# The delta rule's gate taken into the scan, and the scan's norm folded into its transposition

## The chip, the cores and the metric

The kernel runs on one core of a Trainium2 chip. The time is the device time of one launch in microseconds, the median over runs. The core has five engines with queues of their own, each worked through strictly in order: PE (TensorE: matmuls and transpositions), DVE (VectorE), ACT (ScalarE), POOL (GpSimd) and SP, which here only issues DMAs (ACT issues some as well). Engines wait for each other through semaphores. Matmul results land in PSUM, eight banks of 128x512 fp32; everything else lives in SBUF or, where it is parked, in DRAM.

## The reference, cut to what matters

One layer of a generator over 256 latent and 256 context tokens of width 1024: a SwiGLU half step, a mixer, a second half step, a last norm. The change is in the mixer, which runs a gated delta rule (8 heads of 128, both directions) and a Mamba-2 state-space scan (SSD, 32 heads of 64 in two groups) on one input projection, and merges them:

```python
def mixer_out(f, o, y, ...):
    ya = rmsnorm(o, gdn_norm_g) * silu(za)                  # delta rule: norm and gate
    yb = (y + mb_d * xs) * silu(zB)                         # SSD: skip and gate
    yb = rmsnorm(yb, mb_norm_g)                             # per group of 1024 channels
    merged = sigmoid(ga) * (ya @ w_branch_gdn) + sigmoid(gb) * (yb @ w_branch_mb)
    return merged @ w_out
```

## The kernel before

The program is written as a list of steps (`PLAN`), each with a priority; a scheduler at build time puts the instructions of each engine into one fixed order by priority, by readiness in its own timing model and by free buffers. What stands on a queue stays in that order on the chip. A step that comes earlier in `PLAN` is also served first when buffers of a pool are handed out; a lower number ahead of a step is more urgent.

Weight products are done as three fp32r matmuls of split operands: `unit` loads 512 KB of weights into one of four `raw` buffers (SP), casts the high part `whi` (ACT, L197) and subtracts for the low part `wlo` (DVE, L201); `mm3` (L212 to L214) multiplies. Projections whose input is `hF` run as plain fp32 matmuls (L648, L1165) straight from `raw`.

The steps that matter, in the order of `PLAN`:

- `zB1`, `zA9`, `zB4`: gate projections as plain fp32 matmuls. `zA_gen` makes eight tiles `zth` (L648 on PE, L1178 on ACT, L1179 on DVE) and parks each in DRAM as `zAsc`. `zB_gen` makes four blocks `zbt` (L1165, L1168, L1169), parked as `zsc`.
- `h40` is `ssd_all`, the scan, four quarters (two groups, two halves). Per quarter `ssd_off` loads `xlat`, starts `y` as skip term (L1455) and adds four products `pyo` through `yo` (L1466 to L1472); `ssd_diag`, twice, builds an 8x128 decay matrix in `Es` (POOL L1501, DVE L1503, ACT L1505), a second one B (L1509 on ACT or L1511 on DVE, by `DGB`, then L1514), multiplies both (L1516) and sends them through PE as `pyd` (L1519, added in L1520); `ssd_gate` loads the parked `zt`, multiplies (L1528) and squares on ACT with a row sum (L1529). After each second quarter `ssd_norm` makes the factor `yr` and scales `y` in four passes (L1540).
- `y0`, `y1` are `ssd_out`: `y` is transposed on PE into `pyb` (L1574, one PSUM bank), the norm's gain applied and the result split into `ybH` (ACT, L1578) and `ybL` (DVE, L1579).
- `gdn_out`: the normed delta-rule output `o` is transposed (`pya`, L1400), multiplied with the loaded `zA` (L1405), split into `yaH` (ACT) and `yaL` (POOL, L1407), and goes through eight projections with `wbg`, 24 matmuls each.
- `mb_out`: eight projections of both `yb` groups with `wbm`, then `w_out`.

Of the kernel before, what the change touches and what calls it, by code (L numbers as in the profile page):

```python
# [8 lines left out]
AF = mybir.ActivationFunctionType  # L9
ALU = mybir.AluOpType  # L10
# [4 lines left out]
P = 128  # L15
D = 1024
KD = 8
NL = 256
# [10 lines left out]
T4 = 2  # L29
NCV = 2  # L30
PLAN = """10/k3 block_decay k6 18/v3 13/dts 18/g2 20/v2 g3 row_scale 5/elim 20/g10 v4 21/gdn_rows dts_rows 13/m0 14/m1 13/chain_start s0 s1 m2 m3 22/q9
    B_part 27/x17 25/lat_h 22/C_part 30/g17 chain_out 13/s2 s3 14/gdn_norm 15/ssd_pre 30/zB1 zA9 zB4 15/h40 51/y0 gdn_out y1 70/mb_out"""
NG = 5
GQ = 0
EST = ("t4", "tt")
# [4 lines left out]
F2T, W2L, HUT = ["mm", "mm", "mg", "mg", "tr", "ch"], "dve", "tZ"  # L40
CBT = "n8"
WAT = [("tt", "tt"), ("tt", "tt"), ("c4", "c4"), ("ring", "ring"), ("s4", "s4"), ("s4", "s4"), ("tt", "tt"), ("c4", "c4")]
DGA, DGB, DGM = "g", "av", "v"
PYD = ("sd", "tr")
XDT = "c4"
YOT = 'tA'
# [90 lines left out]
class Kernel:  # L137
# [1249 lines left out]
        for t in range(2):  # L1387
            V.tensor_tensor(o[t], o[t], bc(rs[:, t], 8, P), op=ALU.mult)

    def gdn_out(self):  # L1390

        nc, V = self.nc, self.nc.vector
        o, bc = self.o, self.bc
        yH = Ks(self, 8, NL, "yaH")
        yL = Ks(self, 8, NL, "yaL")
        for h2 in range(4):
            pv = self.smp([P, 2, NL], "pya", "ch")
            for j in range(2):
                for t in range(2):
                    nc.tensor.transpose(pv[:, j, t * P:t * P + P], o[t][:, 2 * h2 + j], self.ident)  # L1400
            ya = self.t2([P, 2, NL], "ya")
            j, hs = h2 // 2, slice(2 * (h2 % 2), 2 * (h2 % 2) + 2)
            zA = self.t2([P, 2, NL], "zA", tag="tL")
            nc.sync.dma_start(zA, self.zAsc[2 * h2:2 * h2 + 2].rearrange("m p n -> p m n"))
            V.scalar_tensor_tensor(out=ya, in0=pv, scalar=self.gng, in1=zA, op0=ALU.mult, op1=ALU.mult)  # L1405
            nc.scalar.copy(yH.t[j][:, hs], ya)
            (V if YAL[h2] == "v" else nc.gpsimd).tensor_tensor(yL.t[j][:, hs], ya, yH.t[j].bitcast(F32)[:, hs], op=ALU.subtract)  # L1407
        mg = self.mg = Ks(self, 8, NL, "mg", F32)
        for m in range(8):
            acc = self.proj("wbg", m, yH, yL, NL)  # L1410
            ga = self.t2([P, NL], "ga", tag="tL")
            nc.sync.dma_start(ga, self.gsc[m])
            V.scalar_tensor_tensor(out=mg[m], in0=ga, scalar=1.0, in1=acc, op0=ALU.add, op1=ALU.mult)
# [117 lines left out]
    def ssd_norm(self, gi):  # L1531
        V = self.nc.vector
        r = self.const([P, 2], f"yr{gi}")
        V.tensor_tensor(r, self.rsum[:, :, gi, 0], self.rsum[:, :, gi, 1], op=ALU.add)

        self.rsqrt(r, r, 1.0 / 1024, 4 * EPS)
        for hf in range(2):
            y = self.yx[gi, hf][0]
            for t in range(2):
                V.tensor_scalar(out=y[:, t], in0=y[:, t], scalar1=r[:, t:t + 1], scalar2=None, op0=ALU.mult)  # L1540

    def ssd_all(self):

        self.yx = {}
        self.v3 = lambda ap: ap.rearrange("p (h c) -> p h c", c=64)
        self.b64 = lambda ap: ap.rearrange("p (h o) -> p h o", o=1).to_broadcast([P, ap.shape[1], 64])
        qs = [(gi, hf) for gi in range(2) for hf in range(2)]
        self.ssd_off(*qs[0])
        yield
        for n, q in enumerate(qs):  # L1550
            for i in range(2):
                self.ssd_diag(*q, i)
                yield
                yield
                if i == OFA and n < 3:
                    self.ssd_off(*qs[n + 1])
                    yield
            self.ssd_gate(*q)
            if q[1]:
                self.ssd_norm(q[0])  # L1560
            yield

    def ssd_out(self, gi):

        nc, V = self.nc, self.nc.vector
        y = [self.yx[gi, hf][0] for hf in range(2)]
        yH = Ks(self, 8, NL, f"ybH{gi}")
        yL = Ks(self, 8, NL, f"ybL{gi}")
        for c2 in range(4):
            pv = self.smp([P, 2, NL], "pyb", "tr")  # L1570
            for j in range(2):
                c = 2 * c2 + j
                for t in range(2):
                    nc.tensor.transpose(pv[:, j, t * P:t * P + P], y[c // 4][:, t, (c % 4) * P:(c % 4) * P + P], self.ident)  # L1574
            for j in range(2):
                c = 2 * c2 + j
                g = self.mbg[:, 8 * gi + c:8 * gi + c + 1]
                nc.scalar.activation(yH[c], pv[:, j], AF.Identity, scale=g)  # L1578
                V.scalar_tensor_tensor(out=yL[c], in0=pv[:, j], scalar=g, in1=yH[c].bitcast(F32), op0=ALU.mult, op1=ALU.subtract)  # L1579
        self.yb.append((yH, yL))  # L1580
# [124 lines left out]
```

## Time and profile before

| | us |
|---|---|
| median of 3 runs | 1290.8 (1288.43 to 1293.3) |
| the profiled execution, its own time | 1292.01 |
| its span in the trace | 1290.3 |
| PE busy | 1247.7 (97%) |
| DVE busy | 954.3 (74%) |
| ACT busy | 481.3 (37%) |
| POOL busy | 98.8 (8%) |
| mean granted TensorE clock | 0.981 |

The times of the profile are microseconds from the span's start. Busy is the union of an engine's instructions; a matmul's end is modelled, so that neighbours overlap a little. The stretch of the change lies between 865 us, where the first `zA` projections run, and 1016 us, where `mb_out` starts. Plain fp32 matmuls are recorded in two passes, so that one of them counts as two in the trace; transpositions and fp32r matmuls count once.

### The profile page before, as it was taken

The numbers are of one execution on the slowest core, as the hardware profiler recorded it, in microseconds if no ns is written. First come the engines' busy times: TensorE is split into PE (matmuls) and PEld (weight loads), VectorE is DVE, ScalarE is ACT, GpSimd is POOL, SyncE is SP. The second block draws the span as 40 slices with busy tenths as digits, with TensorE's granted clock in tenths as the row PEclk, the third lists the DMA queues.
The fourth block names the chain that finished last, engine by engine and source line by source line (L and its number), as shares of the span: only waits on it lengthen the run. The fifth ranks groups of instructions, "written<-read, shape, count | busy, mean of one in ns | idle before, by whom it ended". The sixth has DMA issues, their size and how long they took to land.

```text
span 1290.3 us, 21033 instructions
## 1 busy us (share of the span) xinstructions
PE 1247.7 (97%) x8042; PEld 1088.3 (84%) x8042; DVE 954.3 (74%) x1748; ACT 481.3 (37%) x919; POOL 98.8 (8%) x119
## 2 busy tenths in 40 slices
PE   9999999999999999998989999999996999999997
PEld 8888888888899888888978799867545999999997
DVE  5997586646667995888786798948896566866565
ACT  4321222212236663144323554422224445543443
POOL 1000000000010140100110211100111002000000
PEclk9999999999998999999999999999997999999998
DMA  9566367636632388885541456668655565555552
GB/s 366 181 221 212 115 222 240 206 129 219 214 104 106 107 202 201 263 249 163 158 121 50 143 176 192 198 201 291 221 178 168 188 224 180 196 193 180 181 183 78
DMA packets 138132, 239.41 MB, mean 186 GB/s; under 512 B 41072, under 2 KB 81456, under 8 KB 137904
## 3 DMA queue, kind: packets, MB, share of 16 engines
q1 hardware_dynamic: 98688, 214.32, 51.1%
q10 hardware_dynamic: 39344, 23.76, 6.2%
q8 instruction: 63, 1.03, 0.3%
q14 instruction: 37, 0.30, 0.1%
HBM read 211.72 MB, written 26.31 MB: 184 GB/s over the span
## 4 chain that ended last, share of the span: by engine, by line
PE 61%; issue 16%; DVE 12%; DMA 7%; ACT 2%; SPq 1%; POOL 0%; POOLq 0%; DVEq 0%; ACTq 0%
PE acc L213 16%; PE acc L212 16%; PE acc L214 16%; PE acc L648 3%; DVE wlo L201 1%; DVE cv L667 1%; DVE Es L1503 1%; PE acc L1165 1%; PE pada L318 1%; DVE Es L1514 1%; PE pn L1343 1%; DMA vsc<-vt 1%; DVE N L1056 1%; DVE etmp L1053 1%; DMA raw<-in_wgs 1%
## 5 line engine op out<-in xcount | busy, mean ns | idle before, releaser
L197 ACT CAST whi<-raw 128x1024 fp32r<-128x1024 f32 (+1 forms) x208 | 214.5, 1034 | 454.9 <-PE acc L213 374.8
L213 PE MATMUL acc<-hL,whi 128*128 128x512 f32 (+1 forms) x976 | 345.1, 354 | 0.5 <-DVE hL L468 0.5
L214 PE MATMUL acc<-hH,wlo 128*128 128x512 f32 (+1 forms) x976 | 344.5, 353 | 0.0
L212 PE MATMUL acc<-hH,whi 128*128 128x512 f32 (+1 forms) x976 | 339.9, 355 | 0.9 <-ACT cv L665 0.5
L201 DVE TENSOR_TENSOR wlo<-raw,whi 128x1024 fp32r<-128x1024 f32 (+1 forms) x208 | 250.7, 1207 | 73.8 <-ACT whi L197 72.2
L212 PEld LDWEIGHTS acc<-hH,whi 128*128 128x128 f32 x976 | 186.1, 191 | 24.7 <-ACT cv L665 1.1
L213 PEld LDWEIGHTS acc<-hL,whi 128*128 128x128 f32 x976 | 186.6, 191 | 23.9 <-DVE hL L468 0.9
L214 PEld LDWEIGHTS acc<-hH,wlo 128*128 128x128 f32 x976 | 186.5, 191 | 23.3
L290 DVE CUSTOM_DVE_ANT_0 junk<-wadat,cs 128x1024 f32<-128x1024 f32 x80 | 97.8, 1222 | 43.5 <-DMA wadat<-in_wadaT 42.6
L213 PE MATMUL acc<-aL,whi 128*128 128x256 f32 (+1 forms) x384 | 122.9, 323 | 0.0
L214 PE MATMUL acc<-aH,wlo 128*128 128x256 f32 (+1 forms) x384 | 122.3, 323 | 0.0
L212 PE MATMUL acc<-aH,whi 128*128 128x256 f32 (+1 forms) x384 | 122.2, 323 | 0.0
L667 DVE SCALAR_TENSOR_TENSOR cv<-cbuf,cc,cv 128x512 f32<-128x512 f32 (+1 forms) x144 | 97.9, 690 | 8.8 <-ACT cv L665 7.2
L648 PE MATMUL acc<-hF,raw 128*128 128x256 f32 x416 | 93.1, 380 | 1.9 <-DMA raw<-in_wg 1.7
L648 PEld LDWEIGHTS acc<-hF,raw 128*128 128x128 f32 x416 | 78.2, 190 | 14.9 <-issue 2.4
L213 PEld LDWEIGHTS acc<-aL,whi 128*128 128x128 f32 x384 | 73.0, 190 | 5.7
L212 PEld LDWEIGHTS acc<-aH,whi 128*128 128x128 f32 x384 | 72.6, 190 | 5.7
L214 PEld LDWEIGHTS acc<-aH,wlo 128*128 128x128 f32 x384 | 72.7, 190 | 5.5
L604 DVE SCALAR_TENSOR_TENSOR xl<-acc,hg,xl 128x256 f32<-128x256 f32 x64 | 30.3, 482 | 47.3 <-PE acc L214 46.8
L1165 PE MATMUL acc<-raw,hF 128*128 128x512 f32 x128 | 58.3, 607 | 0.0
L1165 PEld LDWEIGHTS acc<-raw,hF 128*128 128x128 f32 x128 | 24.7, 195 | 29.9 <-issue 29.6
L401 POOL TENSOR_TENSOR sqa<-sqa,sqb 128x256 f32<-128x256 f32 x12 | 11.3, 945 | 455.4 <-ACT sqb L399 452.6
(403 smaller groups left out, 1971.8 us busy)
## 6 DMA issues: line engine op xcount, KB each, us to landing
raw<-in_wgu SPq DMA_DIRECT2D x76, 512.0 KB, 4.0
wadat<-in_wadaT SPq DMA_DIRECT2D x56, 512.0 KB, 4.1
raw<-in_wdn SPq DMA_DIRECT2D x44, 512.0 KB, 3.4
wada<-in_wada SPq DMA_DIRECT2D x16, 512.0 KB, 9.6
raw<-in_wg SPq DMA_DIRECT2D x16, 512.0 KB, 4.6
Es<-asd SPq DMA_DIRECT2D x16, 512.0 KB, 4.4
raw<-in_wxs SPq DMA_DIRECT2D x16, 512.0 KB, 3.7
raw<-in_wzB SPq DMA_DIRECT2D x16, 512.0 KB, 3.9
```

What stands on the lines that cost most here:

```text
L197: nc.scalar.copy(hi, raw)
L201: engs[i % len(engs)].tensor_tensor(lo[:, c:c + w], raw[:, c:c + w], hi[:, c:c + w].bitcast(F32), op=ALU.subtract)
L212: mm(acc, wh, xh, start=start, stop=False)
L213: mm(acc, wh, xl, start=False, stop=False)
L214: mm(acc, wl, xh, start=False, stop=stop)
L290: self.nc.vector.tensor_tensor_reduce(out=self.junk, in0=w, in1=self.cs[s], scale=1.0, scalar=0.0, op0=ALU.mult, op1=ALU.add, accum_out=out)
L318: mm = lambda c, q: nc.tensor.matmul(pa[:, c], loads[k][c][:, q * P:q * P + P], self.cTs[:, q:q + 1].to_broadcast([P, P // 2, 2]), start=q ...
L604: nc.vector.scalar_tensor_tensor(out=xs, in0=acc[:, NL * s - g0:NL * s - g0 + NL], scalar=hg[s][:, m:m + 1], in1=xs, op0=ALU.mult, op1=ALU ...
L648: self.nc.tensor.matmul(acc, w[:, k * P:k * P + P], self.hF[:, k], start=k == 0, stop=k == KD - 1)
L667: nc.vector.scalar_tensor_tensor(out=u3, in0=buf[:, 0:R, j:j + 64], scalar=cw[:, j:j + 1], in1=u3, op0=ALU.mult, op1=ALU.add)
L1053: V.tensor_tensor(tmp, N[:, :, k + 1:32, k:k + 1].to_broadcast([P, 2, nr, k]), N[:, :, k:k + 1, 0:k].to_broadcast([P, 2, nr, k]), op=ALU.mult)
L1165: nc.tensor.matmul(accs[t], self.hF[:, k, sl], w[:, wsl], start=k == 0, stop=k == 7)
```

## The change

Four edits. `gdn_out` is cut in two: `gdn_pre` (transposition, gate and split of the delta rule's output) moves to a place between `zA9` and `zB4` in `PLAN`, ahead of the scan `h40`; the eight projections keep the name `gdn_out` and come after `y1`. The scan's norm no longer scales `y` on DVE: `ssd_norm` makes a diagonal matrix `ydg` of the factors on ACT, and `ssd_out` multiplies `y` with it instead of transposing against the identity, so that scaling and transposition are one plain fp32 matmul. `pyb` alternates between two PSUM banks. And all eight B matrices are started on ACT (`DGB` is "a" and not "av").

```diff
-    ... 30/zB1 zA9 zB4 15/h40 51/y0 gdn_out y1 70/mb_out"""
+    ... 30/zB1 zA9 29/gdn_pre 30/zB4 15/h40 51/y0 y1 60/gdn_out 70/mb_out"""
-DGA, DGB, DGM = "g", "av", "v"
+DGA, DGB, DGM = "g", "a", "v"
@@ def gdn_out(self), now gdn_pre up to the split of ya
-    def gdn_out(self):
+    def gdn_pre(self):
         yH = Ks(self, 8, NL, "yaH")
         yL = Ks(self, 8, NL, "yaL")
+        self.ya = yH, yL
...
+    def gdn_out(self):
         mg = self.mg = Ks(self, 8, NL, "mg", F32)
         for m in range(8):
-            acc = self.proj("wbg", m, yH, yL, NL)
+            acc = self.proj("wbg", m, *self.ya, NL)
@@ def ssd_norm(self, gi)
         self.rsqrt(r, r, 1.0 / 1024, 4 * EPS)
-        for hf in range(2):
-            y = self.yx[gi, hf][0]
-            for t in range(2):
-                V.tensor_scalar(out=y[:, t], in0=y[:, t], scalar1=r[:, t:t + 1], scalar2=None, op0=ALU.mult)
+        dg = self.t2([P, 2, P], "ydg", tag="tM")
+        for t in range(2):
+            self.nc.scalar.activation(dg[:, t], self.ident, AF.Copy, scale=r[:, t:t + 1])
+        self.ydg[gi] = dg
@@ def ssd_out(self, gi)
-            pv = self.smp([P, 2, NL], "pyb", "tr")
+            pv = self.smp([P, 2, NL], "pyb", ("tr", "sd")[c2 % 2])
...
-                    nc.tensor.transpose(pv[:, j, t * P:t * P + P], y[c // 4][:, t, (c % 4) * P:(c % 4) * P + P], self.ident)
+                    nc.tensor.matmul(pv[:, j, t * P:t * P + P], y[c // 4][:, t, (c % 4) * P:(c % 4) * P + P], self.ydg[gi][:, t],
+                                     start=True, stop=True)
```

The scheduler makes a new order of it. Three places of it follow; in the changed kernel line numbers past L1390 are some 5 to 7 higher.

DVE, where the scan starts, before: the start of `y` (L1455), the first `yo` and the first decay matrices stand between the gates `zth` of the `zA` projections.

```order
L1169 SCALAR_TENSOR_TENSOR zbt<-zbt,acc 128x512 x2
L1455 TENSOR_TENSOR yg<-xlat,mbD 128x512 x2
L1471 TENSOR_TENSOR yo<-pyo,cbm 128x512
L1132 TENSOR_TENSOR sst<-pSs,egm 128x256
L1472 TENSOR_TENSOR yg<-yg,yo 128x512
L1179 SCALAR_TENSOR_TENSOR zth<-zth,acc 128x256 x2
L1437 TENSOR_TENSOR cbm<-pcb,UT 128x2x128
L1511 TENSOR_TENSOR Es<-cbm,dt 128x1024
```

DVE at the same place now: the gate of the delta rule (`ya`, L1406) stands behind the `zth`, and all of `yo` and `yg` behind `ya`.

```order
L1179 SCALAR_TENSOR_TENSOR zth<-zth,acc 128x256 x2
L1406 SCALAR_TENSOR_TENSOR ya<-pya,cc,zA 128x512 x2
L1179 SCALAR_TENSOR_TENSOR zth<-zth,acc 128x256
L1406 SCALAR_TENSOR_TENSOR ya<-pya,cc,zA 128x512 x2
L1476 TENSOR_TENSOR yo<-pyo,cbm 128x512 x2
L1460 TENSOR_TENSOR yg<-xlat,mbD 128x512 x2
L1477 TENSOR_TENSOR yg<-yg,yo 128x512 x2
L1460 TENSOR_TENSOR yg<-xlat,mbD 128x512 x2
```

What moved: every `yo` and `yg` of the scan is now queued behind the last `ya`, which needs the last two of the eight `zA` tiles back from DRAM.

SP's DMA queue, before, around the first weights of `zA`: three of the four `xlat` loads stand ahead of the `zA` weights.

```order
L1453 DMA xlat<-xsc 128x2x512
L638 DMA raw<-in_wBC 128x1024
L1450 DMA Sm<-ssc 128x2x512
L638 DMA raw<-in_wg 128x1024
L1450 DMA S_7930<-ssc 128x2x512
L1488 DMA Es<-asd 128x1024
L638 DMA raw<-in_wzB 128x1024
L1453 DMA xlat<-xsc 128x2x512 x2
```

SP's queue now, behind the last weights of `zA`: the loads of `zA` back from DRAM and the `xlat` loads behind them.

```order
L638 DMA raw<-in_wzA 128x1024
L1493 DMA Es<-asd 128x1024
L638 DMA raw<-in_wzB 128x1024
L1405 DMA zA<-zAsc 128x2x256
L638 DMA raw<-in_wzB 128x1024 x2
L1405 DMA zA<-zAsc 128x2x256
L638 DMA raw<-in_wzB 128x1024
L1405 DMA zA<-zAsc 128x2x256
L1458 DMA xlat<-xsc 128x2x512
L1532 DMA zt<-zsc 128x512 x2
L1458 DMA xlat<-xsc 128x2x512 x2
```

What moved: all four `xlat` loads are issued behind the last load of `zA`, which waits for the store of the eighth tile.

PE at the scan's end, before: the last zB matmuls and the last scan products `pyd`, then the transpositions `pya` and `pyb`, then the first `wbg` matmuls.

```order
L1165 MATMUL acc<-raw,hF 128x512
L1519 MATMUL pyd<-xlat,Es 128x64 x16
L1165 MATMUL acc<-raw,hF 128x512 x23
L1519 MATMUL pyd<-xlat,Es 128x64 x16
L1400 MATMUL pya<-ident,o_7186 128x128
L1400 MATMUL pya<-ident,o_7187 128x128
L1400 MATMUL pya<-ident,o_7186 128x128
```

PE there now: 48 `wbg` matmuls, two of the eight projections, are threaded between the last scan products; behind the last `pyd` come all eight groups of `pyb` in one row, then the other six projections.

```order
L212 MATMUL acc<-yaH,whi 128x256
L213 MATMUL acc<-yaL,whi 128x256
L214 MATMUL acc<-yaH,wlo 128x256
L1524 MATMUL pyd<-xlat,Es 128x64 x16
L1580 MATMUL pyb<-ydg,yg 128x128 x32
L212 MATMUL acc<-yaH,whi 128x256
L213 MATMUL acc<-yaL,whi 128x256
L214 MATMUL acc<-yaH,wlo 128x256
```

What moved: before, the second group's `pyb` were spread between `wbg` and `wbm` matmuls that covered their splitting; now 144 `wbg` matmuls wait on PE's queue behind both groups' `pyb`.

More of the change, by code (lines that the diff above doesn't have):

```diff
@@ L31 @@
 PLAN = """10/k3 block_decay k6 18/v3 13/dts 18/g2 20/v2 g3 row_scale 5/elim 20/g10 v4 21/gdn_rows dts_rows 13/m0 14/m1 13/chain_start s0 s1 m2 m3 22/q9
-    B_part 27/x17 25/lat_h 22/C_part 30/g17 chain_out 13/s2 s3 14/gdn_norm 15/ssd_pre 30/zB1 zA9 zB4 15/h40 51/y0 gdn_out y1 70/mb_out"""
+    B_part 27/x17 25/lat_h 22/C_part 30/g17 chain_out 13/s2 s3 14/gdn_norm 15/ssd_pre 30/zB1 zA9 29/gdn_pre 30/zB4 15/h40 51/y0 y1 60/gdn_out 70/mb_out"""
 NG = 5
@@ L1407, in gdn_out @@
             (V if YAL[h2] == "v" else nc.gpsimd).tensor_tensor(yL.t[j][:, hs], ya, yH.t[j].bitcast(F32)[:, hs], op=ALU.subtract)
+    def gdn_out(self):
+        nc, V = self.nc, self.nc.vector
         mg = self.mg = Ks(self, 8, NL, "mg", F32)
         for m in range(8):
-            acc = self.proj("wbg", m, yH, yL, NL)
+            acc = self.proj("wbg", m, *self.ya, NL)
             ga = self.t2([P, NL], "ga", tag="tL")
@@ L1536, in ssd_norm @@
         self.rsqrt(r, r, 1.0 / 1024, 4 * EPS)
-        for hf in range(2):
-            y = self.yx[gi, hf][0]
-            for t in range(2):
-                V.tensor_scalar(out=y[:, t], in0=y[:, t], scalar1=r[:, t:t + 1], scalar2=None, op0=ALU.mult)
+        dg = self.t2([P, 2, P], "ydg", tag="tM")
+        for t in range(2):
+            self.nc.scalar.activation(dg[:, t], self.ident, AF.Copy, scale=r[:, t:t + 1])
+        self.ydg[gi] = dg
     def ssd_all(self):
-        self.yx = {}
+        self.yx, self.ydg = {}, {}
         self.v3 = lambda ap: ap.rearrange("p (h c) -> p h c", c=64)
```

## The prediction

> **What bounds the kernel now.** I began with the busy shares, then the waits of PE between 838 and 1012 us, then windows across the scan and its end, then single instructions at the edges.
>
> ```profile
> PE 1247.7 (97%) x8042; PEld 1088.3 (84%) x8042; DVE 954.3 (74%) x1748; ACT 481.3 (37%) x919; POOL 98.8 (8%) x119
> ```
>
> PE is busy for 97%, so a gain can only come from the few places where it stands still, or from work taken off it. Around the change it waits for this (us in total, times, longest):
>
> ```profile
> PE pyb L1574 <- DVE ybL L1579: 7.2, 2, 5.0
> PE pyd L1519 <- DVE Es L1516: 1.9, 1, 1.9
> PE pya L1400 <- DVE ya L1405: 1.4, 1, 1.4
> ```
>
> Windows (start:end, length, busy of PE, PEld, DVE, ACT, POOL, then the granted clock, DMA share, GB/s):
>
> ```profile
> 871.94:969.50 97.56, 95.69 (x353) 58.60 (x352) 88.49 (x194) 26.77 (x66) 12.63 (x7) 0.98 0.67 227
> 975.00:980.00 5.00, 1.57 (x11) 0.89 (x9) 1.74 (x4) 1.42 (x3) 0.00 (x0) 0.94 0.72 233
> 980.00:985.00 5.00, 0.70 (x4) 0.71 (x4) 2.60 (x6) 1.81 (x5) 0.14 (x1) 0.50 0.34 124
> 985.00:990.00 5.00, 2.86 (x12) 2.18 (x11) 4.05 (x7) 1.37 (x3) 2.09 (x2) 0.50 0.47 137
> 990.00:993.00 3.00, 3.00 (x16) 3.00 (x15) 1.40 (x3) 1.44 (x3) 1.92 (x2) 0.50 0.45 136
> 1000.00:1010.00 10.00, 10.00 (x85) 10.00 (x85) 6.01 (x9) 4.15 (x5) 0.00 (x0) 1.00 0.76 253
> ```
>
> Through the scan PE is full (95.69 of 97.56) and DVE nearly (88.49). The gap is 975 to 988, and behind it PE works at half clock until 993. Its edges on PE:
>
> ```profile
> 864.92 1.24 PE L648 MATMUL acc<-hF,raw 128*128 128x256 f32 x5
> 908.24 3.60 PE L1165 MATMUL acc<-raw,hF 128*128 128x512 f32 x8
> 969.81 3.68 PE L1519 MATMUL pyd<-xlat,Es 128*128 128x64 f32 x32
> 984.30 1.09 PE L1574 MATMUL pyb<-ident,yg 128*128 128x128 f32 x4 [4.98 <-DVE ybL L1579]
> 1015.05 0.60 PE L1574 MATMUL pyb<-ident,yg 128*128 128x128 f32 x4
> 1015.41 0.36 PE L212 MATMUL acc<-ybH,whi 128*128 128x256 f32 x1
> ```
>
> The last scan products end at 973.5. `mb_out` starts at 1015.4, and as one more `pyb` group of 0.6 follows later, I compare with 1016.0. On DVE, the scan's start, its last product and its last gate:
>
> ```profile
> 871.94 1.29 DVE L1455 TENSOR_TENSOR yg<-xlat,mbD 128x512 f32<-128x512 f32 x2 [5.50 <-DMA xlat<-xsc]
> 968.29 1.22 DVE L1516 TENSOR_TENSOR Es<-Es 128x1024 f32<-128x1024 f32 x1
> 981.77 0.69 DVE L1528 TENSOR_TENSOR yg<-yg,zt 128x512 f32<-128x512 f32 x1 [3.23 <-DMA zt<-zsc]
> ```
>
> So the last gate waits for the last block of `zB` to come back from DRAM, and norm, four scalings and the splits of `pyb` through a single bank follow one after another. The last decay product ends at 969.5; I call that moment L.
>
> **The change part by part.** The rows it is priced by, grouped over 865 to 992 us (busy, mean ns of one | idle before):
>
> ```profile
> L1514 DVE SCALAR_TENSOR_TENSOR Es<-cbm,dt,Es 128x128 f32<-128x128 f32 x64 | 19.5, 368 | 0.1
> L1503 DVE SCALAR_TENSOR_TENSOR Es<-Es,gc 128x128 f32<-128x128 f32 x48 | 15.5, 386 | 0.0
> L1472 DVE TENSOR_TENSOR yg<-yg,yo 128x512 f32<-128x512 f32 x16 | 12.7, 794 | 0.2
> L1471 DVE TENSOR_TENSOR yo<-pyo,cbm 128x512 f32<-128x512 f32 x16 | 10.8, 682 | 0.4 <-PE pyo L1469 0.4
> L1509 ACT ACTIVATE Es<-cbm,dt 128x128 f32<-128x128 f32 x32 | 10.2, 389 | 8.2 <-DVE Es L1503 8.1
> L1516 DVE TENSOR_TENSOR Es<-Es 128x1024 f32<-128x1024 f32 x8 | 9.6, 1215 | 0.0
> L1469 PE MATMUL pyo<-xo,cbm 128*128 128x512 f32 x16 | 8.2, 592 | 0.0
> L1540 DVE TENSOR_SCALAR yg<-yg,yr 128x512 f32<-128x512 f32 x8 | 6.0, 809 | 0.0
> L1520 DVE TENSOR_TENSOR yg<-yg,pyd 128x512 f32<-128x512 f32 x8 | 5.3, 679 | 1.3 <-PE pyd L1519 1.3
> L1529 ACT ACTIVATE zt<-yg 128x512 f32<-128x512 f32 x8 | 5.0, 630 | 29.5 <-DVE yg L1528 29.0 <-ACT zt L1529 0.5
> L1511 DVE TENSOR_TENSOR Es<-cbm,dt 128x1024 f32<-128x1024 f32 x4 | 4.9, 1216 | 0.0
> L201 DVE TENSOR_TENSOR wlo<-raw,whi 128x1024 fp32r<-128x1024 f32 x3 | 3.7, 1220 | 0.9 <-ACT whi L197 0.9
> L1579 DVE SCALAR_TENSOR_TENSOR ybL<-pyb,cc,ybH 128x256 fp32r<-128x256 f32 x6 | 2.9, 478 | 1.9 <-ACT ybH L1578 1.8
> L1578 ACT ACTIVATE ybH<-pyb,cc 128x256 fp32r<-128x256 f32 x6 | 2.8, 470 | 8.7 <-PE pyb L1574 5.8 <-DVE ybL L1579 2.9
> L1405 DVE SCALAR_TENSOR_TENSOR ya<-pya,cc,zA 128x512 f32<-128x512 f32 x3 | 2.1, 741 | 1.2 <-DMA zA<-zAsc 1.2
> L1129 PE MATMUL pSs<-xw,BC 128*128 128x128 f32 x8 | 1.1, 275 | 0.0
> ```
>
> *`gdn_pre` ahead of the scan.* By DVE's new order no `yo` or `yg` runs before the fourth `ya`, and by SP's the four `xlat` loads stand behind the last `zA` load. So the scan's start on DVE hangs on the eighth `zA` tile, its store and its load. The `zA` projections ended at 908.2; 16 recorded `pyo` matmuls (0.51 each, 8.2) and 32 `pyd` (3.7) now come later, a group of `pya` (0.5) earlier: 896.8. Gate in ACT and DVE with handoffs about 1.7 (estimate). Then, by the DMA issues and the store's spread (us to landing; minimum, median, maximum over these stores and loads):
>
> ```profile
> raw<-in_wbg SPq DMA_DIRECT2D x8, 512.0 KB, 3.5
> zAsc<-zth ACTq DMA_DIRECT2D x8, 128.0 KB, 5.0
> zA<-zAsc SPq DMA_DIRECT2D x4, 256.0 KB, 2.7
> ```
>
> ```profile
> DMA to landing us min/median/max: 1.7/4.0/6.4
> ```
>
> With 4.0 for the store (the middle between 1.7 and 6.4), 2.7 for the load and 0.74 for `ya`, DVE starts the scan's `yo` at 906 (1.7 to 6.4 gives 904 to 908), 34 us later than at 871.9. PE's zB matmuls have no part in that wait and run meanwhile.
>
> *DVE's work from there to L.* 48 L1503, 15.5; 48 of the 64 L1514, 14.6 (the first two matrices are made before); 6 of the 8 L1516, 7.2; L1471 10.8; L1472 12.7; 26 other operations of 128x512 at 0.68, 17.7; five L201 for the `wbg` weights that are now split amid the scan, 6.1. Sum 84.6. The sum of the same kind over the stretch before is 94 (L1514, L1503, L1472, L1471, L1516 and L1511, 73.0; some 31 operations of 0.68, 21.1) against 88.49 busy, since neighbours overlap: times 0.94, 79.6. Idle: none at one end, at the other the 9.1 that DVE idled before; I take 4, as nothing of the DVE rows waits long. L = 906 + 79.6 + 4 = 990 (977 with bare spacings and no wait, 997 with slow stores and the idle of before). The edit `DGB` takes L1511 (4.9) off DVE, already left out above, and adds 32 L1509 to ACT, 10.2: hidden, since ACT is busy 26.77 of 97.56. The norm takes L1540 off DVE (6.0), but only the half of it behind the second norm (3.0) stood at the end.
>
> *PE's own floor.* 973.5, less the 1.9 wait for `Es`, plus 16 `pya` (0.6 for four, 2.4), plus the two `wbg` projections threaded in, 48 matmuls at 10.00/85 = 0.118, 5.7: the last `pyd` can't end before 979.7, L not before 978. So DVE, not PE, sets L by 12 us.
>
> *The tail.* Behind L: `pyd` 1.8 (half of the 3.68 row), L1520 0.68, gate 0.69, square 0.63, then sums, factors and two diagonals on ACT, about 2.3 (estimate from the smaller rows): second `ydg` at L + 6.1. The diagonal stands on ACT behind the first `ybH`, so all but the first split wait for it. `pyb` then goes in four pairs over two banks. As plain matmul a group has eight records, 1.1 by the nearest row of that shape (L1129), against 0.6 as transposition. A pair takes 1.1 for the first group (the second lies beside it), three splits on ACT 1.4, one on DVE 0.48 and handoffs 0.2: 3.2. Three such turns until the last pair is through PE: L + 15.7. Only then come the 144 `wbg` matmuls behind them, 17.0, and as PE has idled, 5.6 us of them at half clock (as from 987.5 to 993 before), 2.8. `mb_out` starts at 990 + 15.7 + 17.0 + 2.8 = 1025.5 against 1016.0: **+9.5 us**. The two banks and the saved scalings are inside this sum; what is late next is the row of splits, which before lay beside `wbg` matmuls.
>
> Before 865 and behind `mb_out` nothing changes but neighbours in full queues; I put that at nothing, covered by PE's own work.
>
> *A rule against the trace.* From 980 to 993 the clock is 0.50 behind a window with 1.57 busy of 5. The Trainium skill, "TensorE: Matmul & The Clock Gate", Part 4: PE-mode transpose, says that transpose-mode matmuls do not count as busy for the clock gate in the way of others. By it `pyb` as plain matmuls would keep the clock up in the tail, and the 2.8 (up to 4.8 with the pairs' own slowing, an estimate) would go; in the trace before, all such groups at half clock stand beside real gaps, so it can't tell.
>
> **The rivals.**
>
> *PE stays the bound* (the other side). If neighbours on DVE overlap as bare spacings do, and store and load come at once, L lies at 978 to 980.5. The tail then gives 1013.5 to 1016.0, with a full clock 2.8 less: -5.3 to 0, 1285.5 to 1291. It decides at L = 980.5, that is, DVE 9.5 us faster than my sum. For it: DVE sheds 4.9 and 3.0; against it: 34 us of later start while DVE was 88.49 of 97.56 busy.
>
> *Weight splits stall the scan's queues.* Five splits of `wbg` weights now stand on ACT and DVE between decay matrices. Their `raw` buffers are freed by zB matmuls on PE, then take 3.5 to load. If PE is late with one, DVE stands for load and split each time; two such turns of 3.5 give +7 on L: 1307. Against it: these waits would hide where DVE is behind PE anyway.
>
> *The clock stays up in the tail.* PE then has 64 plain `pyb` records there with gaps of about 2 us, where before it stood still for 5.0 in one piece; and 975 to 980 ran at 0.94 with only 1.57 busy. That takes 2.8 to 4.8 (the 2.8, and half of four groups of 1.1 that would run at half rate) off the forecast: 1295 to 1297. Against it: a busy share like that was followed by 0.50 in the next window. By the rule just cited this is how it goes.
>
> **How the numbers follow.** The profiled execution took 1292.0, 1.2 above the median 1290.8, so +9.5 is 1301.5 against it and 1300 against the median. Chances: forecast 0.45, PE as the bound 0.22, splits 0.18, clock 0.10, and 0.05 for small gains on PE that I put at nothing. The range reaches down to near the middle of the PE case, 1287, and up to the bound L = 997 with 3 us for slow `pyb`, 16.5 + 3 = +19.5, 1310. The likeliest case's own range is 1296 to 1306. A run can't tell less than 0.5% (6.5 us) from no change. Faster (below 1284.3) 0.11: 0.06 of the PE case, whose lower end is 1.2 from that line, and the 0.05. The same 0.30: 0.16 of the PE case, 0.08 of the clock case, 0.06 of the forecast's lower edge. Slower (above 1297.3) 0.59: the rest.
>
> **What would show it.** Right: DVE's first `yo` at 904 to 908 behind a wait for `zA`; the last product for `Es` (L1516 before) near 990; PE waiting for `Es` for about 10 us in all before the last `pyd`; `pyb` groups in pairs with some 3 us between, PE mostly idle for 12 us; then `wbg` in one block and `mb_out` near 1025. Wrong: `yo` well before 904, or the last product before 981 with PE full, or `pyb` at two groups a microsecond; or a long DVE wait behind L201, which makes it worse.

## The result: slower by about 1.3%

| | before | changed |
|---|---|---|
| median of the runs, us | 1292.05 (1288.43 to 1295.57) | 1304.52 (1303.16 to 1317.25) |
| profiled execution, us | 1292.01 | 1305.73 |
| its span, us | 1290.3 | 1304.0 |

The ratio of the times, formed from undisturbed runs, is 1.0126, 95% interval 1.0094 to 1.0158; the medians alone give 1.0097. 12.5 us between the medians stand against the 9.5 us forecast, and 1304.5 lies inside the range. By the ratio the change costs some 16 us (12 to 20 by its interval), which the distances in the table below bear out. The waits of PE in the same stretch, changed kernel (in `gdn_pre` its line numbers are one higher than before, behind it 5 to 7):

```profile
PE pyd L1524 <- DVE Es L1521: 11.1, 1, 11.1
PE pyb L1580 <- DVE ybL L1586: 5.2, 3, 2.1
PE pyo L1471 <- DVE yo L1476: 2.6, 1, 2.6
PE acc L212 <- DVE mg L1418: 1.4, 1, 1.4
```

Before, the longest wait was 5.0 for `ybL`. Now PE stands 11.1 us for the last scan products' matrix. PE's instructions around it (start, length):

```profile
896.85 12.28 PE L1165 MATMUL acc<-raw,hF 128*128 128x512 f32 x28 [0.47 <-DVE ya L1406]
...
911.55 2.12 PE L1524 MATMUL pyd<-xlat,Es 128*128 128x64 f32 x18
...
968.20 3.67 PE L1524 MATMUL pyd<-xlat,Es 128*128 128x64 f32 x16
...
977.13 1.90 PE L1524 MATMUL pyd<-xlat,Es 128*128 128x64 f32 x16
...
991.24 7.06 PE L1524 MATMUL pyd<-xlat,Es 128*128 128x64 f32 x32 [11.09 <-DVE Es L1521]
998.09 3.73 PE L1580 MATMUL pyb<-ydg,yg 128*128 128x128 f32 x16
1003.88 2.02 PE L1580 MATMUL pyb<-ydg,yg 128*128 128x128 f32 x16 [2.06 <-DVE ybL L1586]
1007.47 2.02 PE L1580 MATMUL pyb<-ydg,yg 128*128 128x128 f32 x16 [1.57 <-DVE ybL L1586]
1011.06 2.02 PE L1580 MATMUL pyb<-ydg,yg 128*128 128x128 f32 x16 [1.57 <-DVE ybL L1586]
...
1031.88 0.28 PE L212 MATMUL acc<-ybH,whi 128*128 128x256 f32 x1
```

The four pairs of `pyb` are there, the last three 3.59 us apart, and `mb_out` starts at 1031.9. On DVE, the last gate `ya`, the scan's first `yo`, the wait for a weight split and the last product:

```profile
901.67 0.75 DVE L1406 SCALAR_TENSOR_TENSOR ya<-pya,cc,zA 128x512 f32<-128x512 f32 x1 [4.88 <-DMA zA<-zAsc]
902.34 1.28 DVE L1476 TENSOR_TENSOR yo<-pyo,cbm 128x512 f32<-128x512 f32 x2
...
948.21 1.22 DVE L201 TENSOR_TENSOR wlo<-raw,whi 128x1024 fp32r<-128x1024 f32 x1 [3.80 <-ACT whi L197]
...
993.23 1.22 DVE L1521 TENSOR_TENSOR Es<-Es 128x1024 f32<-128x1024 f32 x1
```

Windows of the changed kernel, with PE's busy time first and the granted clock third from the end:

```profile
902.34:994.45 92.11, 77.63 (x285) 46.40 (x284) 81.38 (x168) 34.16 (x80) 16.47 (x8) 0.89 0.67 229
```

```profile
968.00:975.00 7.00, 6.85 (x30) 6.29 (x30) 7.00 (x16) 1.74 (x3) 0.75 (x1) 0.52 0.68 246
...
985.00:990.00 5.00, 0.00 (x0) 0.00 (x0) 5.00 (x14) 2.57 (x9) 1.32 (x1) 0.50 0.47 146
991.00:998.00 7.00, 6.76 (x32) 6.80 (x33) 4.79 (x12) 1.26 (x4) 0.00 (x0) 0.50 0.01 2
998.00:1002.00 4.00, 3.82 (x18) 3.52 (x17) 2.19 (x5) 1.31 (x4) 0.71 (x1) 0.50 0.21 55
1003.00:1014.00 11.00, 6.07 (x48) 5.58 (x48) 5.75 (x13) 5.55 (x13) 0.00 (x0) 1.00 0.00 0
...
1015.00:1030.00 15.00, 15.00 (x128) 15.00 (x127) 7.56 (x11) 5.11 (x5) 0.00 (x0) 1.00 0.51 164
```

DVE is busy for 81.38 of the 92.11 us from the first `yo` to the last product; the clock is low twice, and back at 1.00 from 1003.

Executions differ by some us ahead of the change too (the first `zB` matmul starts between 842 and 849 us in all profiles but those of kernels 10 and 12, which have another order ahead of it). The table therefore gives, besides the ratio, two distances within each profile, read from the first starts of the tiles' instructions: from the first `zB` matmul to the start of the last `Es` product, and to the first matmul of `w_out`, which stands behind everything that the change touches. The medians are differences to before in the same session.

| kernel | ratio to before (95%) | medians, us | to last `Es` product | to `w_out` |
|---|---|---|---|---|
| before | 1 | | 120.2 | 216.4 |
| changed | 1.0126 (1.0094 to 1.0158) | +12.5 | 147.7 | 232.5 |
| 1 move alone | 1.0190 (1.0159 to 1.0220) | +24.4 | 150.6 | 247.0 |
| 2 other edits alone | 0.9984 (0.9966 to 1.0002) | -2.0 | 119.0 | 215.0 |
| 3 `y1` late | 1.0108 (1.0078 to 1.0138) | +14.5 | 147.7 | 231.2 |
| 4 `gdn_pre` behind `y0` | 0.9998 (0.9978 to 1.0018) | +0.4 | 122.9 | 217.7 |
| 5 `gdn_pre` behind the scan | 1.0038 (1.0024 to 1.0052) | +5.6 | 118.9 | 221.2 |
| 6 old norm | 1.0135 (1.0115 to 1.0154) | +17.0 | 148.4 | 233.9 |
| 7 splits on POOL | 1.0156 (1.0133 to 1.0179) | +19.5 | 149.6 | 236.0 |
| 8 `zA` early | 1.0123 (1.0099 to 1.0147) | +14.7 | 144.8 | 232.0 |
| 9 more `Es` buffers | 1.0030 (1.0018 to 1.0043) | +4.3 | 116.4 | 221.5 |
| 10 before, more buffers | 1.0090 (1.0074 to 1.0106) | +12.3 | 88.3 | 223.5 |
| 11 wbg ahead of y | 1.0007 (0.9989 to 1.0024) | +0.4 | 122.0 | 219.2 |
| 12 both | 1.0039 (1.0027 to 1.0052) | +5.5 | 83.3 | 218.7 |

### The profile page after: what moved, and what is told of

Same layout as the page of the kernel before. It is cut to its first block, busy times and chain, and to the rows that moved or that the text cites. A ratio compares the mean times of both kernels' runs of the same rounds, so it can differ in the third digit from the quotient of the medians.

```text
span 1304.0 us, 21117 instructions
## 1 busy us (share of the span) xinstructions
PE 1251.0 (96%) x8074; PEld 1092.7 (84%) x8074; DVE 947.7 (73%) x1736; ACT 492.7 (38%) x955; POOL 102.9 (8%) x119
## 5 line engine op out<-in xcount | busy, mean ns | idle before, releaser
L213 PE MATMUL acc<-aL,whi 128*128 128x256 f32 (+1 forms) x384 | 122.9, 323 | 0.0
```

Of the source, the lines that this page charges most:

```text
L213: mm(acc, wh, xl, start=False, stop=False)
```

## Experiments

**Which edit costs.** First the move alone (scalings, transpositions, one bank and `DGB` as before; its edit is shown against the kernel before), then the other edits alone. From here on an edit is shown against the changed kernel, unless said otherwise.

```diff
-    ... zA9 zB4 15/h40 51/y0 gdn_out y1 70/mb_out
+    ... zA9 29/gdn_pre 30/zB4 15/h40 51/y0 y1 60/gdn_out 70/mb_out
```

> The move of gdn_pre ahead of the scan, alone: scalings on DVE, transpositions against the identity, one PSUM bank and the mix of ACT and DVE for the B matrices stay as before. Theory A (the move costs: DVE starts the scan late, and the splits of both groups lie bare behind the last pyd): first yo at 902 to 906, PE waits about 10 us for Es, mb_out 13 to 20 us later than before, slower by 13 to 20 us. Theory B (the plain-fp32 products with the diagonal and their pairs over two banks cost): the order at the scan's start moves but the time is within 5 us of before.

```diff
-    ... zA9 29/gdn_pre 30/zB4 15/h40 51/y0 y1 60/gdn_out 70/mb_out
+    ... zA9 zB4 15/h40 51/y0 gdn_pre gdn_out y1 70/mb_out
```

> The other three edits alone (norm in the transposition, two banks, all B matrices started on ACT), gdn_pre where it was, behind y0. Theory A: the chain at the scan's end gets shorter by the scalings and by the second bank, PE's 7.2 us wait for ybL falls to under 4; faster by 2 to 6 us. Theory B: the plain matmuls take 1.0 instead of 0.6 a group and the tail grows; slower by 3 to 10 us.

The move alone costs more than the whole change, +24.4 us, and more than the 13 to 20 expected of it. The others alone bring nothing that the interval separates from zero (-4.4 to +0.3 us): PE's wait for `ybL` fell from 7.2 to 2.1 us as expected, but its waits for `pya` grew from 1.9 to 5.6. PE's waits with the move alone, and two of its eight `pyb` groups:

```profile
PE pyd L1524 <- DVE Es L1521: 15.4, 2, 14.4
PE pyb L1580 <- DVE ybL L1585: 14.8, 6, 3.8
```

```profile
1010.64 1.09 PE L1580 MATMUL pyb<-ident,yg 128*128 128x128 f32 x4 [2.20 <-DVE ybL L1585]
1013.93 1.08 PE L1580 MATMUL pyb<-ident,yg 128*128 128x128 f32 x4 [2.20 <-DVE ybL L1585]
```

Through one bank a group takes 3.29 us, and six turns stand in the row (the eighth group comes behind the first `wbg`); two banks send two groups in 3.59. So the norm's new form, the second bank and `DGB` do earn 8 to 14 us in the order that the move makes, where the row lies bare (8 by the ratios, 12 by the medians, 14.5 to `w_out`), and some 2 in the old order, which the interval does not separate from zero. Kernel 6, further down, has the second bank and `DGB` but the old norm: of the 14.5 us it has 13.1, so the norm's form is worth little. Theory B is out.

**Is it the bare row?**

```diff
-    51/y0 y1 60/gdn_out 70/mb_out
+    51/y0 60/gdn_out 51/y1 70/mb_out
```

> The changed kernel with one thing different: the projections of the delta rule's branch stand ahead of y1 in the plan, so that PE has 24 and then 117 of its matmuls between the second group's pyb. Theory A (uncovered splits cost): two of the four turns of 3.6 us get a cover, mb_out 6 to 8 us earlier than in the changed kernel, +6 to +8 us against before. Theory C (the lost time is all in the wait for the last Es and the low clock behind it; splits would be waited for in any place): within 2 us of the changed kernel, +12 to +15.

The cover works as an order and saves next to nothing: 231.2 against 232.5. Its windows:

```profile
993.00:1000.00 7.00, 7.00 (x33) 7.00 (x34) 4.48 (x11) 0.95 (x3) 0.00 (x0) 0.50 0.03 8
1004.00:1006.00 2.00, 0.43 (x4) 0.46 (x5) 1.31 (x3) 1.35 (x4) 0.00 (x0) 1.00 0.00 0
1007.00:1013.00 6.00, 4.59 (x22) 4.29 (x21) 2.41 (x6) 1.52 (x4) 0.00 (x0) 0.50 0.15 44
```

From the end of the last product to `mb_out`, PE stands idle for 3.6 us instead of 6.6, so the cover does work; but PE is busy for 1.8 us more, since the clock fell a second time, at 1007, and the first covering `wbg` matmuls ran at half rate, where in the changed kernel all 144 ran at 1.00. Theory A had also priced a turn at its whole 3.6 us, of which PE stands idle for only 1.6 to 2.1; the rest is `pyb` itself. Theory C had the time right, but not its reason: the splits were covered in part.

**Is it the late start?** Two kernels start the scan where it was, a third starts it a little earlier.

```diff
-    zA9 29/gdn_pre 30/zB4 15/h40 51/y0 y1 60/gdn_out 70/mb_out
+    zA9 zB4 15/h40 51/y0 29/gdn_pre 60/gdn_out 51/y1 70/mb_out
```

> The changed kernel with gdn_pre and the projections behind y0 and ahead of y1, where they stood before, the new priority numbers kept; against the kernel with the other three edits alone it differs by these priorities and by where the last pyb stand. Theory A: DVE's scan starts near 872 as before, no wait of 10 us for Es, -6 to 0 us against before. Theory B: as the changed kernel, +8 to +15.

```diff
+    zA9 zB4 15/h40 29/gdn_pre 51/y0 y1 60/gdn_out 70/mb_out
```

> The changed kernel with gdn_pre written behind the scan in the plan (same priority 29), y0, y1 and the projections as in the changed kernel: the scan claims queues and buffers first again, while the second group's four pyb groups still stand in one row ahead of 144 wbg matmuls. Theory A1 (the late start of the scan is the cost): first yo near 874, last Es product near 970, no long wait for Es, within -4 to +4 us of before. Theory A2 (the uncovered row of pyb is the cost): +6 to +12 us.

In both the last product stands within 3 us of before's place, and 12 and 7 of the 12.5 microseconds are gone (to `w_out`, 14.8 and 11.3 of 16.1). In the second one, the row of the second group's `pyb` is still bare and PE waits 9.3 us in a place of its own:

```profile
PE pya L1401 <- DVE ya L1406: 9.3, 1, 9.3
PE pya L1401 <- DVE zbt L1169: 3.2, 1, 3.2
PE pyb L1580 <- DVE ybL L1586: 2.8, 3, 1.3
```

Its +5.6 us (3.1 to 6.7 by the interval) lie between what A1 and A2 said. So the late start carries the larger part, and what is left belongs to the scan's end.

```diff
-            nc.sync.dma_start(zA, self.zAsc[2 * h2:2 * h2 + 2]...)
+            nc.sync.dma_start(zA, self.zAsc[0:2]...)
```

> The changed kernel with all four loads of zA reading the first two parked tiles (the other six are stored and left unused, so the gate is computed with the wrong tiles): the last ya no longer waits for a tile that has just been stored. Theory A1: yo starts 4 to 5 us earlier (897 to 898) and the last Es product with it, 3 to 5 us off the changed kernel's time. Rival (the slack behind the start, 10.7 us of DVE idle time, swallows it): within 1.5 us of the changed kernel.

A smaller dose than meant: `ya` now waited 2.6 us for another load, and `yo` began 2.2 us earlier, counted from the first `zB` matmul. The last product came 2.9 us earlier, `w_out` 0.5. It does not decide anything by time; a shift of the start does reach the last product.

**Why does the start pass to the end?** My sum said: DVE's work. Five splits moved from DVE to POOL were to test that.

```diff
-            acc = self.proj("wbg", m, *self.ya, NL)
+            acc = self.proj("wbg", m, *self.ya, NL, "pool" if m < 5 else "dve")
```

> The changed kernel with the low parts of the first five wbg weight blocks made on POOL instead of DVE (five L201 of 1.2 us, and DVE's wait of 3.8 us for one of them, leave DVE's queue in the scan). Theory A1 (DVE's work from its late start to the last Es product sets the end): the last product 6 to 9 us earlier, so much off the time against the changed kernel, +5 to +8 against before. Rival (loads of Es and POOL's own pace set it): within 2 us of the changed kernel.

The last product came no earlier (149.6 against 147.7), and `w_out` came 3.5 us later, more than the rival allowed. PE's wait for `Es` grew to 14.5. But the edit did not relieve DVE. Here are the stretches from the first `yo` to the end of the last product in kernel 7, in kernel 1, in kernel 2 and in the kernel before (busy of PE first, of DVE third):

```profile
899.68:993.54 93.86, 74.94 (x278) 43.77 (x277) 83.61 (x163) 33.97 (x80) 26.24 (x13) 0.90 0.64 225
903.18:997.87 94.69, 75.54 (x288) 44.23 (x286) 84.94 (x176) 26.48 (x54) 15.32 (x8) 0.91 0.65 223
873.35:968.84 95.49, 94.86 (x363) 58.83 (x361) 79.67 (x184) 36.12 (x98) 12.13 (x7) 1.00 0.67 226
873.15:969.51 96.36, 94.50 (x347) 57.55 (x346) 87.29 (x193) 26.78 (x66) 12.63 (x7) 0.98 0.67 226
```

In kernel 7 DVE is busy for 83.6 us, against 81.4 in the changed kernel. The splits (6.1) have left its queue, but nine other operations (five in the changed kernel) took 1.3 to 2.4 us each, instead of 0.34 to 0.69, and every one of them ran beside an operation on POOL, as here:

```profile
975.59 2.82 POOL L201 TENSOR_TENSOR wlo<-raw,whi 128x1024 fp32r<-128x1024 f32 x1
...
976.70 1.86 DVE L1508 SCALAR_TENSOR_TENSOR Es<-Es,gc 128x128 f32<-128x128 f32 x1
978.38 1.93 POOL L1506 TENSOR_TENSOR Es<-Es,gc 128x1024 f32<-128x1024 f32 x1
978.48 2.38 DVE L1533 TENSOR_TENSOR yg<-yg,zt 128x512 f32<-128x512 f32 x1
```

That POOL is what held them is inferred from this. So kernel 7 is no test of a lighter DVE: DVE had 2.2 us more to do, and the last product came 1.9 us later. In kernel 1, where the scalings and half of the B matrices stay on DVE, it had 3.6 us more, and the product came 2.9 later. PE is busy for only 75 to 78 us in these three. That fits an end that DVE's work sets. In the old order it is otherwise: kernel 2 has 7.6 us less of DVE's work than before, and its last product moved by 1.2 us; PE is full there, 94.9 of 95.5.

SP's queue shows a second limit. The last two loads of `Es`, changed kernel:

```profile
971.90 0.33 SPq L1493 DMA_DIRECT2D Es<-asd  x1
...
979.06 0.33 SPq L1493 DMA_DIRECT2D Es<-asd  x1
```

They follow the ends of the third quarter's `pyd` (968.20 + 3.67 = 971.87; 977.13 + 1.90 = 979.03) to within 0.03 us. There are two buffers for the first decay matrix, so a quarter can't load its own before the quarter before has gone through PE: the quarters form a ring. From that load to the product it is then 18.0 and 14.2 us (989.88 and 993.23) through load, POOL, DVE, ACT and DVE again. In that time DVE hardly stands still: it is busy for 20.1 of the 21.3 us from the first of these loads to the last product. So four buffers:

```diff
-EST = ("t4", "tt")
+EST = ("t4", "tt", "c4", "tt")
```

> The changed kernel with four buffers instead of two for the first decay matrix (every second one in two buffers that stand free by then); the order on all queues shifts with it. Theory A3 (a quarter of the scan takes 24 to 28 us because its loads of Es wait for the pyd of the quarter before, whatever DVE has to do; the late start then shifts all four): the last Es product 10 to 20 us earlier than 994, no wait of 10 us, -3 to +6 us against before. Theory A1 (DVE's sum of work from its late start): within 4 us of the changed kernel, +9 to +15.

The last product comes 31 us earlier than in the changed kernel (116.4 against 147.7), more than expected, and the time falls from +12.5 to +4.3. Its last load, the row of products, and the stretch from its first `yo` to the end of the last product:

```profile
929.59 0.32 SPq L1493 DMA_DIRECT2D Es<-asd  x1
```

```profile
L1521 DVE TENSOR_TENSOR Es<-Es x8: 1209/1218/1222, 874.4 to 960.6; 128x1024 f32<-128x1024 f32 x8
```

```profile
902.87:961.79 58.92, 57.18 (x203) 30.92 (x203) 52.73 (x115) 19.56 (x49) 11.35 (x5) 1.00 0.65 221
```

So the buffers matter, and much, and theory A1 in the form given, with the same work in the stretch, is out. But this does not part theory A3 from DVE's work, for the work in the stretch is not the same: DVE is busy in it for 52.7 us instead of 81.4, and of the 33.2 us by which it is shorter, 28.7 are DVE's (PE is now all but full in it, 57.2 of 58.9). With four buffers four of the eight matrices are made ahead of the first `yo`, not two, and the five splits and a quarter of `yo` and `yg` come behind the last product. What is shown is that the loads wait for their buffers and that two buffers keep matrix work behind the late start. Whether the ring of four quarters would be any faster with the same work on DVE, no run tells.

Of 31 us only 11 reach `w_out`: now the last gate is late (DVE waits 4.2 for `zt` to come back and gates at 987.1 and 988.8), and PE stands 6.5 us for `ybL` ahead of the second group.

**Does that pay in the kernel before, and does cover for the end?** The edit of kernel 10 is the same line, in the kernel before.

> The kernel before with the same four buffers. Theory A3: the scan's quarters come faster than 25 us apart and the last pyd is done before the last zB block; what PE waits for at the scan's end is then the zB block's way through DRAM, the norm and the splits, which stays: 0 to -4 us. If nothing paced the scan: within 1 us of before with the quarters 25 us apart.

Neither: slower by 12.3 us. The scan was through at 88.3 instead of 120.2, but its earlier work stands ahead of the `zA` and `zB` projections and their gates. The last `zA` tanh moved from 910.5 to 931.3 us, the last `zB` matmul from 969.4 to 983.2, the last gate from 982.9 to 995.2. Of that, 6.0 us lie ahead of the first `zB` matmul (854.1 against 848.1), whose place the new order moves as well. So in the kernel before, a scan that is through 32 us sooner brings nothing by itself: the last gate still waits for the last `zB` block.

```diff
-    zA9 29/gdn_pre 30/zB4 15/h40 51/y0 y1 60/gdn_out 70/mb_out
+    zA9 zB4 15/h40 51/gdn_pre gdn_out y0 y1 70/mb_out
```

> The changed kernel with gdn_pre and the eight projections behind the scan and ahead of both y0 and y1 (all at 51): the scan starts as before, and PE has all 192 wbg matmuls (22.7 us) to do while the last gate, the norm and the splits run. If the gap at the scan's end is a lack of ready work on PE: PE's waits between 965 and 1016 fall from some 11 us to under 6, -3 to -8 us against before. If ya itself comes too late (its loads and pya stand behind the last zB block): within 2 us of before.

> The kernel of the run before with the four buffers for the decay matrix as well. If the pacing of the scan and the lack of ready work at its end are two separate costs, both gains add: -5 to -10 us against before, the fastest of all. If the last zB block's way through DRAM sets the end in both, the buffers bring nothing: as the run before within 1.5 us.

Kernel 11 equals before, as the second theory had it. PE waits as long as ever at the scan's end, now for `ya`:

```profile
PE pya L1401 <- DVE ya L1406: 8.1, 1, 8.1
PE pya L1401 <- DVE zbt L1169: 3.0, 1, 3.0
```

Kernel 12 (with the buffers) is 5.5 us slower than before, which neither theory said. From the first `zB` matmul to `w_out` it takes what kernel 11 takes (218.7 against 219.2); the loss lies ahead of that, where its order differs and the first `zB` matmul comes at 849.9 instead of 842.4. No kernel of the study is faster than before by more than its interval.

**The clock in the row.** The changed kernel's order with transpositions and scalings instead of products with the diagonal:

```diff
-                    nc.tensor.matmul(pv[...], y[...], self.ydg[gi][:, t], start=True, stop=True)
+                    nc.tensor.transpose(pv[...], y[...], self.ident)
```

> The changed kernel with the norm's scaling back on DVE and pyb as transpositions against the identity; two banks and the order kept, so the row of four turns at the end stands as in the changed kernel. Scaling adds some 3 us ahead of the second group, a group takes less on PE. If transpositions count for the granted clock like plain matmuls, the clock comes back about 4 us into the row, as in the changed kernel (1002), and the time is 0 to 4 us above the changed kernel. If they do not, the clock stays at 0.50 through the row and some 4 to 6 us into the wbg matmuls: 4 to 10 us above it.

```profile
992.00:999.00 7.00, 6.65 (x32) 6.68 (x33) 4.91 (x12) 1.72 (x4) 0.00 (x0) 0.50 0.06 23
999.00:1002.00 3.00, 2.31 (x10) 1.58 (x10) 2.08 (x5) 1.53 (x5) 0.00 (x0) 0.50 0.16 44
1003.00:1014.00 11.00, 6.06 (x24) 4.57 (x24) 6.28 (x15) 4.86 (x12) 0.00 (x0) 0.50 0.03 9
```

In the row PE is as busy as in the changed kernel (6.06 against 6.07 of 11) at 0.50 instead of 1.00. Yet the time is little above the changed kernel (1.4 us to `w_out`, 1.2 by the ratios, 4.5 by the medians of two sessions), since a transposed group takes less: the last pairs stand 3.51 us apart even so.

## Why the prediction was right, and where it was not

The runs bear out the path that the prediction named: the move makes DVE start the scan late (shown by kernels 1, 4 and 5), DVE's work from there sets the last product (it fits the traces, but no run isolates it), and the splits then lie bare (kernel 1). That the sum came within a few microseconds is luck in part, since terms were off in both directions.

- *The late start*: forecast 906, measured 902.3. As the changed kernel was 2.6 us ahead at the first `zB` matmul (845.5 against 848.1), that is 905 in before's time. Right.
- *DVE's work to L*: forecast 990, measured 994.4, which is 997 in before's time. The work was priced well, 79.6 against 81.4 busy; the idle time was too small, 4 against 10.7. Of it 3.8 are the wait for one split, 3.1 waits for POOL's part of `Es`, 2.1 for `xlat` and 1.0 for `pyd`. That DVE sets L in the new order fits kernels 1 and 7, as told above. The argument for it did not hold: "DVE was 88.49 of 97.56 busy" says little, since in that order 7.6 us less of DVE's work left L where it was (kernel 2). And the sum has no word on why so much of the work must lie behind the late start: two buffers hold the loads back. They did so before as well: in before's trace, whose rows follow, the last two loads of `Es` start at 945.0 and some 3.5 later, where the third quarter's `pyd` end (942.72 + 1.90 and 946.48 + 2.00).

```profile
942.72 1.90 PE L1519 MATMUL pyd<-xlat,Es 128*128 128x64 f32 x16
...
946.48 2.00 PE L1519 MATMUL pyd<-xlat,Es 128*128 128x64 f32 x16 [1.86 <-DVE Es L1516]
```

```profile
944.99 3.85 SPq L1488 DMA_DIRECT2D Es<-asd  x2
```

- *The tail*: forecast L + 15.7 until the last pair is through PE, measured 18.6 (994.45 to 1013.08). Two terms were too small. Behind the wait stood 32 `pyd`, not 16, and they ran at half clock: 7.06 us in all, of which 3.9 lie behind L, against 1.8 in the sum. And a turn takes 3.59, not 3.2.
- *The half clock on `wbg`* (2.8) did not come; the 144 ran at 1.00. That is the clock rival's effect, paid ahead instead, on `pyd`.
- *The baseline*: by the way from `mb_out` to `w_out`, before's start was worth 1018.4, not 1016.0 (1064.5 less the 46.1 us that this way takes in the changed kernel), since two more `pyb` groups followed, not one, with what PE waits for them. From 1018.4 to 1031.9 makes 13.5; with the forecast's 9.5 the difference is L +4.4, tail and `wbg` +1.9 (37.4 against 35.5), baseline -2.4.
- *PE stays the bound*: it did not, L is far above 980.5. *Splits stall the queues*: one wait of 3.8 us is in the trace, where the rival had two of 3.5; what it costs by itself no run shows.
- *The rule that transpositions do not count for the clock* (the Trainium skill, "TensorE: Matmul & The Clock Gate", Part 4: PE-mode transpose): kernel 6 agrees, 0.50 against 1.00 at the same busy share. It isn't isolated: the plain row began with 3.73 us without a gap, the transposed one with 2.11.

Open: why kernel 8 saves less at `w_out` than at its own step; and how the loss behind the late start is divided between DVE's work and the ring of loads.

## What to carry to other kernels

A nearly full engine isn't shown to be the limit until work taken off it moves the end, and an edit meant to take work off must be seen to do so: five splits left DVE's queue here, and its busy time grew. When more buffers make something faster, look also at which work they let run earlier. A load that waits for a buffer is found by setting its start beside the end of the work that frees it. When a step is put ahead of another in a scheduler's list, look at what now stands behind its last instruction on each in-order queue; here one gate that waits for a DRAM round trip held the first step of the scan. And an edit is worth what its place makes it: the second bank, together with `DGB`, gave 7 to 13 us (kernels 1 and 6) where the splits lay bare, and nothing clear of noise under cover.

## What was not expected of the hardware

Seven microseconds of dense `pyd` (64 columns, PE 6.76 busy of 7.00) left the clock at 0.50 in the changed kernel, and the same in kernels 3 and 6; the 32 took 7.06 us against 3.68 before. The clock came back at about 1002, behind 3.7 us of plain `pyb` with 128 columns. It then stayed at 1.00 from 1003 to 1014 with PE busy for little more than half the time.

In kernel 7 the nine operations of DVE that ran much longer than their like (up to 2.4 us instead of 0.34 to 0.69) all ran beside one on POOL. The five splits took 2.3 to 2.8 us each on POOL, against 1.2 on DVE, and DVE's other work grew by more than the 6.1 us that they had taken there.
